# A decoder trunk on one core: gates and values of retention heads 1 to 7 as column pairs with seven-product blocks, and the retention's output product in two halves of such pairs

## The chip, the core and the metric

The kernel runs on one core of a Trainium2 chip. The metric is the device time of one execution, in microseconds (us), taken as the median of several runs. The core has a matrix engine (TensorE, PE in the profile; its weight loads are PEld), VectorE (DVE), ScalarE (ACT), GpSimd (POOL), SyncE (SP, which here only issues DMAs) and 16 DMA engines. Each engine takes its instructions in the order in which they stand in its own queue. A DMA is issued by an engine and moves data on its own; SP's DMAs are in queue q1 of the profile, POOL's in q0.

## What is computed

There are 256 tokens of 2048 features, all float32, and two layers: a retention layer with a squared-ReLU MLP, then a latent attention layer (MLA) with another such MLP. The change is in the retention and in what joins it to the MLP. Cut to that:

```python
h = rms_norm(x, norm_mix[0])
proj = h @ w_in                                  # 2048 x 12288
q, k, v, gate = split(proj, [2048, 4096, 8192])  # 8 heads: 256 of q, 256 of k, 512 of v, 512 of gate
q = apply_rope(q, cos, sin); k = apply_rope(k, cos, sin) * 256**-0.5
scores = (q @ k.T) * decay[head]                 # per head, causal
o = rms(scores @ v)                              # per head, over its 512 columns
x = x + (silu(gate) * o) @ w_out                 # 4096 x 2048
x = x + square(relu(rms_norm(x, norm_mlp[0]) @ w1)) @ w2
```
`cos` and `sin` are taken of positions times inverse frequencies.

## The kernel before

Tokens stand in two tiles of 128. Every float32 product is made of three matmuls of a rounded format (fp32r): an operand is split into a high and a low part, and high x high, high x low and low x high are added up in PSUM. The activations are split once. The weights come from memory in chunks of 1 MB: `stream` (L177) or `quad` (L251) issue the load on SP into one of three `raw` buffers, ACT casts the high half (`wh`, L154), DVE subtracts it for the low half (`wl`, L155), 128 x 1024 at a time, into five buffers each, and PE multiplies.

There are three forms of product. `gemm` (L372) takes a block of 512 output columns, four rows of 128 of the contraction in a chunk, through `piece` (L204, matmuls at L215 to L217). `gemm_t` (L224) makes the transposed q and k of a head (L239, L243). `gemm_pair` (L300) takes two neighbouring column blocks together: one chunk is a 2 x 2 block of weights (two contraction rows by two column blocks), and `quad` multiplies it with the 2 x 2 block of the activations (two token tiles by two contraction rows). A plain block does this in 8 block products, 24 matmuls (L323 to L325). Where the block's index is in `SEVEN = (3, 5, 7)`, it is done by 7 products, 21 matmuls, after a Strassen-Winograd scheme: DVE makes sums of weight blocks (`u`, L283 to L288) and sums of activation blocks must be at hand (`with_sums`, L358). A pair has eight such blocks or more, all added up in PSUM: four banks `acc`, two banks `tp` for p1 and p5, and the double bank `at` for p6 and p7. At its end `pair_out` (L334) copies six banks out on ACT, makes the results on DVE with four operations of 128x512, and hands on every output block as a pair of parts to be added; `summed` (L351) adds them with four more.

The retention runs head by head (L633). Before, each head is `rg` (its gate, `gemm`), `rq` and `rk` (`gemm_t`), `rv` (its values, `gemm`). The weights of a head are eight chunks of 1 MB for `rg` and `rv` and four for `rq` and `rk`. `ret_rope` (L564) turns q and k by a table, `ret_scores` (L584) multiplies them, `ret_out` (L605) multiplies scores and values, normalises, multiplies with the gate and transposes into `y`. After the eight heads `gemm_blocks` (L384) multiplies `y` with the output weights, four column blocks one by one, and `into_next` (L433) adds the result to x, stores x to the DRAM tiles `x_home`, and makes the split and transposed activations of the MLP. The MLP (L680) is made of pairs, four groups of two `u` pairs and two `d` pairs. All `d` pairs but the last group's add their results to `x_home` by accumulating DMAs on POOL's queue (L736); before the last group `x_tiles` (L117) loads x back.

At the start (`start`, L551) the first head's gate product is joined with the loads of the transposed x (`x0t`, L535) and their split. POOL loads the positions and the constants `cst` (L110, L111), then computes the angles of the rotary table (`sincos`, L451), 512 elements wide and some twenty operations long; ACT takes the sine (`tr_sc`, L487), DVE scales it, PE transposes it, and `rope_tab` (L493) is ready for the first head's rotation.

What runs when is set in two steps. The program writes the products one after another, and puts the work that hangs on their results in a queue with due times: `later(n, f)` (L81) runs `f` n chunks of weights later, `tick` counts chunks, `need` runs queued work until an item exists. A scheduler then moves the instructions of each engine by what they wait for. Tiles of one tag share buffers in turn: `f2k` has 14, `act` 24, `us` 2.

Of the kernel before, what the change touches and what calls it, by code (L numbers as in the profile page):

```python
# [20 lines left out]
P = 128  # L21
# [29 lines left out]
def yoco(ctx: ExitStack, tc: tile.TileContext, a):  # L51
# [58 lines left out]
    nc.gpsimd.dma_start(pos_i, a["pos"])  # L110
    nc.gpsimd.dma_start(cst[:, :C_MASK], a["cst"][:, :C_MASK])  # L111
# [35 lines left out]
    def square_sum(src, acc, name):  # L147
        junk = pool.tile([P, 512], BF16, tag="junk", bufs=2, name=f"{name}_sq")
# [151 lines left out]
    def gemm_pair(w, chunk0, act, kinds, name, done):  # L300
# [150 lines left out]
    def sincos(inv, w, name):  # L451

        n = NT * w
        ang = f2k([NT, w], f"{name}_ang")
# [30 lines left out]
        def finish():  # L485
            sc = f2k([2, NT, w], f"{name}_sc")
            nc.scalar.activation(sc.rearrange("p i t w -> p i (t w)"), r, AF.Sin)  # L487
            return sc
# [4 lines left out]
    rope_tab = pool.tile([P, 2, S], F32, tag="us", bufs=2, name="rope_tab")  # L493
# [23 lines left out]
    def scale_tables():  # L517
# [9 lines left out]
        later(1, turn)  # L527


    act0, r0, y_act, ret_sc, mla_sc = [], [], [], [], []  # L530

    def first_inputs(c):
# [5 lines left out]
        act0.append(v)  # L538

# [11 lines left out]
    def start(half):  # L551
        first_inputs(half)
        if half == 0:
            ret_tables()
        if half == 7:
            nc.sync.dma_start(cst[:, C_MASK:], a["cst"][:, C_MASK:])
            nc.sync.dma_start(gpe, a["gpe"])
# [4 lines left out]
            later(20, mla_tables)  # L562

# [41 lines left out]
    def ret_out(h, s, v, gate):  # L605
# [18 lines left out]
        def turn():  # L624
            for k2 in range(2):
                tp = transposed(lambda t, j: ys[t][:, (2 * k2 + j) * P : (2 * k2 + j + 1) * P], f"ytp{h}{k2}")
                yt = act_tile(f"y{h}{k2}")
                split_act(yt, tp)
                y_act.append(yt)

        later(2, turn)

    for h in range(RH):  # L633
        qk, gate, v, s = [], [], [], []
        wait = 7 if h == 0 else 0

        def gated(acc, h=h, gate=gate, wait=wait):
            src = acc
            if wait:
# [4 lines left out]
            def silu():  # L644
                for t in range(NT):
                    g = f2k([512], f"gate{h}{t}")
                    nc.scalar.activation(g, src[t], AF.Silu, scale=r0[t])
                    gate.append(g)

            later(wait, silu)  # L650

        def valued(acc, h=h, v=v, s=s, gate=gate):
            for t in range(NT):
                vh = f2k([512], f"vh{h}{t}", F32R)
                vl = f2k([512], f"vl{h}{t}", F32R)
                split(vh, vl, acc[t], r0[t])
# [421 lines left out]
```

## Time and profile before

| | |
|---|---|
| median of 3 runs | 2529.87 us (2526.89 to 2533.35) |
| profiled execution: its own time | 2532.54 us |
| profiled execution: span | 2530.4 us |
| PE | 2498.0 us busy (99%), 11794 matmuls |
| DVE | 1889.2 us (75%) |
| ACT | 1445.9 us (57%) |
| POOL | 220.6 us (9%) |

Where the stages begin, from the starts of PE's matmuls:

| stage | starts at us | lasts us |
|---|---|---|
| head 0: rg, rq, rk, rv | 5.3, 40.6, 51.8, 63.1 | 35.3, 11.3, 11.3, 27.4 |
| heads 1 to 7: rg, rq, rk, rv each | 90.5 to 583.4 | 24.7, 11.3, 11.3, 23.1 |
| output product (ro) | 583.4 | 179.7 |
| first MLP | 763.1 | 693 |
| MLA | 1456 | 380 |
| second MLP | 1835.8 | 694 |

The time outside the span is 2532.54 - 2530.4 = 2.1 us. In a line of groups or of a timeline, L is the line of the kernel, then come the engine, the operation, `out<-in` by the names of the tiles, their shapes, and after the bar or in brackets the idle time before it and what ended that. A matmul's time in a row is from its start to its modelled end, and matmuls overlap; the cost of one is the distance of two starts.

### The profile page before, as it was taken

The page shows a single profiled execution, that of the slowest core. Times are in us where ns is not written, and L with a number is a line of the kernel's source. Part 1 is how long each engine was busy: PE and PEld are TensorE (multiplying, and loading weights), DVE is VectorE, ACT ScalarE, POOL GpSimd, SP SyncE. Part 2 cuts the span into 40 slices and gives each one's busy share as a digit, 9 for nine tenths or more (in the row PEclk, how much of TensorE's full clock was granted, in tenths as well). Part 3 has the DMA queues.
Part 4 walks back from the last instruction along what each step waited for, and adds up shares of the span by engine and source line. Part 5 has one row for each costly group of instructions (what it writes and reads, how often), then busy time and mean ns, then how long its engine had stood idle before and what let it go on. Part 6 is the DMA issues. An engine that isn't in the chain of part 4 may idle for free.

```text
span 2530.4 us, 31172 instructions
## 1 busy us (share of the span) xinstructions
PE 2498.0 (99%) x11794; PEld 2096.4 (83%) x11794; DVE 1889.2 (75%) x2430; ACT 1445.9 (57%) x1993; POOL 220.6 (9%) x285
## 2 busy tenths in 40 slices
PE   7999999999999999999999999999999999999999
PEld 6888888888888888888878888998888888888787
DVE  6555555554558988889879866887689888898896
ACT  5544444444446656657556666565566566575663
POOL 6300000000000020110110011101000201101100
PEclk9999999999999999999999999999999999999999
DMA  7555455555655586685775555435555856857754
GB/s 264 178 185 181 173 189 182 184 205 190 207 194 189 192 260 203 210 249 192 241 249 188 212 208 179 163 125 200 191 186 191 260 206 219 248 190 223 255 196 165
DMA packets 89814, 513.67 MB, mean 203 GB/s; under 512 B 10528, under 2 KB 11696, under 8 KB 36416
## 3 DMA queue, kind: packets, MB, share of 16 engines
q1 hardware_dynamic: 71136, 471.69, 52.5%
q0 software_dynamic: 18384, 39.94, 7.6%
q8 instruction: 92, 1.51, 0.2%
q14 instruction: 58, 0.48, 0.1%
q10 hardware_dynamic: 144, 0.05, 0.0%
HBM read 478.09 MB, written 33.55 MB: 202 GB/s over the span
## 4 chain that ended last, share of the span: by engine, by line
PE 84%; DVE 8%; DMA 4%; ACT 3%; issue 1%; POOL 1%; SPq 0%; ACTq 0%; DVEq 0%; POOLq 0%
PE u_c L324 6%; PE u_c L325 6%; PE u_c L323 6%; PE d_c L324 5%; PE d_c L325 5%; PE d_c L323 5%; PE rq_acc L243 2%; PE rg_acc L217 2%; PE ro_acc L217 2%; PE ro_acc L215 2%; PE ro_acc L216 2%; PE rg_acc L215 2%; PE rg_acc L216 2%; PE rv_acc L216 2%; PE rv_acc L217 2%; PE rv_acc L215 2%
## 5 line engine op out<-in xcount | busy, mean ns | idle before, releaser
L155 DVE TENSOR_TENSOR u_wl<-u_raw,u_wh 128x1024 fp32r<-128x1024 f32 (+1 forms) x256 | 279.1, 1120 | 46.3 <-ACT u_wh L154 45.8
L155 DVE TENSOR_TENSOR d_wl<-d_raw,d_wh 128x1024 fp32r<-128x1024 f32 (+1 forms) x256 | 283.5, 1133 | 28.1 <-ACT d_wh L154 27.1
L324 PE MATMUL u_c<-u_wl,n 128*128 128x512 f32 x736 | 287.8, 391 | 5.2 <-DVE u_wl L155 5.2
L323 PE MATMUL u_c<-u_wh,n 128*128 128x512 f32 x736 | 288.7, 392 | 0.0
L154 ACT CAST u_wh<-u_raw 128x1024 fp32r<-128x1024 f32 (+1 forms) x256 | 238.6, 977 | 85.2 <-PE u_c L325 34.4
L325 PE MATMUL u_c<-u_wh,n 128*128 128x512 f32 x736 | 287.1, 390 | 0.0
L154 ACT CAST d_wh<-d_raw 128x1024 fp32r<-128x1024 f32 (+1 forms) x256 | 239.6, 991 | 58.0 <-DMA d_raw<-in_mlp_w 28.5
L324 PE MATMUL d_c<-d_wl,hid 128*128 128x512 f32 x644 | 251.5, 391 | 3.8 <-DVE d_wl L155 3.7
L323 PE MATMUL d_c<-d_wh,hid 128*128 128x512 f32 x644 | 252.0, 391 | 0.0
L325 PE MATMUL d_c<-d_wh,hid 128*128 128x512 f32 x644 | 250.8, 389 | 0.0
L154 ACT CAST u_wh<-u_u 128x1024 fp32r<-128x1024 f32 x96 | 98.3, 1048 | 165.2 <-DVE u_u L288 136.3
L154 ACT CAST d_wh<-d_u 128x1024 fp32r<-128x1024 f32 x84 | 84.7, 1047 | 162.9 <-DVE d_u L288 159.0
L324 PEld LDWEIGHTS u_c<-u_wl,n 128*128 128x128 f32 x736 | 138.6, 188 | 35.9 <-DVE u_wl L155 7.8
L325 PEld LDWEIGHTS u_c<-u_wh,n 128*128 128x128 f32 x736 | 138.6, 188 | 28.7
L323 PEld LDWEIGHTS u_c<-u_wh,n 128*128 128x128 f32 x736 | 138.5, 188 | 28.3
L155 DVE TENSOR_TENSOR u_wl<-u_u,u_wh 128x1024 fp32r<-128x1024 f32 x96 | 115.5, 1223 | 46.4 <-ACT u_wh L154 46.4
L324 PEld LDWEIGHTS d_c<-d_wl,hid 128*128 128x128 f32 x644 | 121.0, 188 | 31.2 <-DVE d_wl L155 6.8
L325 PEld LDWEIGHTS d_c<-d_wh,hid 128*128 128x128 f32 x644 | 120.9, 188 | 24.9
L323 PEld LDWEIGHTS d_c<-d_wh,hid 128*128 128x128 f32 x644 | 120.9, 188 | 24.7
L155 DVE TENSOR_TENSOR ro_wl<-ro_raw,ro_wh 128x1024 fp32r<-128x1024 f32 x64 | 78.4, 1225 | 82.1 <-ACT ro_wh L154 81.9
L155 DVE TENSOR_TENSOR rg_wl<-rg_raw,rg_wh 128x1024 fp32r<-128x1024 f32 (+1 forms) x68 | 81.6, 1208 | 62.6 <-ACT rg_wh L154 62.6
L155 DVE TENSOR_TENSOR d_wl<-d_u,d_wh 128x1024 fp32r<-128x1024 f32 x84 | 99.8, 1222 | 36.0 <-ACT d_wh L154 36.0
(378 smaller groups left out, 6217.6 us busy)
## 6 DMA issues: line engine op xcount, KB each, us to landing
u_raw<-in_mlp_w SPq DMA_DIRECT2D x128, 1024.0 KB, 5.5
d_raw<-in_mlp_w SPq DMA_DIRECT2D x112, 1024.0 KB, 4.9
rv_raw<-in_ret_w_gv SPq DMA_DIRECT2D x32, 1024.0 KB, 4.8
ro_raw<-in_ret_w_out SPq DMA_DIRECT2D x32, 1024.0 KB, 4.8
rg_raw<-in_ret_w_gv SPq DMA_DIRECT2D x28, 1024.0 KB, 4.8
uq_raw<-in_mla_w_uq SPq DMA_DIRECT2D x24, 768.0 KB, 4.2
rq_raw<-in_ret_w_qk SPq DMA_DIRECT2D x16, 1024.0 KB, 4.8
rk_raw<-in_ret_w_qk SPq DMA_DIRECT2D x16, 1024.0 KB, 4.8
```

The lines of the kernel that those rows point to most:

```text
L154: nc.scalar.copy(h, src)
L155: nc.vector.tensor_tensor(l, src, h.bitcast(F32), op=ALU.subtract)
L215: nc.tensor.matmul(acc[t], ah, rh, start=k == 0, stop=False)
L216: nc.tensor.matmul(acc[t], ah, rl, start=False, stop=False)
L217: nc.tensor.matmul(acc[t], al, rh, start=False, stop=k == nk - 1)
L243: nc.tensor.matmul(acc[f], wh[:, cols], a.rearrange("p i s -> p (i s)"), start=k == 0, stop=k == nk - 1)
L323: nc.tensor.matmul(dst, ah, bh, start=n == 0, stop=False)
L324: nc.tensor.matmul(dst, ah, bl, start=False, stop=False)
L325: nc.tensor.matmul(dst, al, bh, start=False, stop=n == total[key] - 1)
```

## The change

Six things change. (1) The gate and value columns of heads 1 to 7 are laid side by side, so that one `gemm_pair`, named rp1 to rp7, makes both; blocks 3, 5 and 7 of its eight take seven products. The order in a head is now rq, rk, rp. Head 0 keeps `rg0` and `rv0`. (2) For these blocks the first activations need sums, made by `sum_up` some chunks after the load. (3) The output product is made of pairs, in two halves. The first half takes heads 0 to 3 (ro00, ro01, three seven-product blocks each), is written after rk of head 4, and its results go to `x_home` by accumulating DMAs (`to_home`); the second half (ro10, ro11, two such blocks each) is written after the last head and goes into x (`into_x`). (4) Therefore `x_home` gets x at the start, by eight DMAs from DRAM to DRAM on POOL's queue, and x for the second half comes from `x_home`. (5) `x_tiles` loads x block by block, two chunks apart, in place of all at once. The first `u` pair of the first MLP takes seven products in two blocks in place of three. (6) At the start, `pos_i`, `cst` and `gpe` are loaded on SP after the fourth half chunk of `rg0`; `sincos` is written with the sixth half in place of the first; its buffers are `act` tiles; `rope_tab` has its own buffer; the square sums' scrap buffer is one in place of two; and the table's transposition is due one chunk later.

```diff
--- before.py
+++ after.py
@@ -107,20 +107,33 @@
     nc.gpsimd.memset(neg_half, -0.5)
     warm = small(1, "warm")
     nc.scalar.copy(warm, neg_half[:, 0:1])
-    nc.gpsimd.dma_start(pos_i, a["pos"])
-    nc.gpsimd.dma_start(cst[:, :C_MASK], a["cst"][:, :C_MASK])
 
     dram = ctx.enter_context(tc.tile_pool(name="dr", bufs=1, space=bass.MemoryType.DRAM))
     x_home = [[dram.tile([P, 512], F32, name=f"xh_{t}_{b}") for b in range(NB)] for t in range(NT)]
     x = [[None] * NB for t in range(NT)]
 
-    def x_tiles(home, name):
-
-        for b in range(NB):
+    def x_tiles(name):
+
+
+        def bring(b):
             both = act_tile(f"x_{name}{b}", F32)
             for t in range(NT):
                 x[t][b] = both[:, t].rearrange("p i s -> p (i s)")
-                nc.gpsimd.dma_start(x[t][b], home(t, b))
+                nc.gpsimd.dma_start(x[t][b], x_home[t][b])
+
+        for b in range(NB):
+            later(2 * b, lambda b=b: bring(b))
+
+    def to_home(c, p):
+
+        for j in range(2):
+            for t in range(NT):
+                for part in c[t][j]:
+                    nc.gpsimd.dma_start(x_home[t][2 * p + j], part, accum_op=ALU.add)
+
+    def into_x(done, c, p):
+        for j in range(2):
+            later(2 * j, lambda j=j: done(2 * p + j, [c[t][j] for t in range(NT)]))
 
     def gain(col):
         return gains[:, col : col + 1]
@@ -145,7 +158,7 @@
         return r.rearrange("p (t i h) -> p t i h", t=NT, i=len(sizes))
 
     def square_sum(src, acc, name):
...
             need(act, i + 1)
-            quad(w, chunk0 + i, act[i], mm, f"{name}{i}")
+            v, more = act[i]
+            quad(w, chunk0 + i, (v, more if kinds[i] else None), mm, f"{name}{i}")
...
+        def f2k(shape, name):
+            return shaped(act_tile(name, F32).rearrange("p j i s -> p (j i s)"), shape)
...
-    rope_tab = pool.tile([P, 2, S], F32, tag="us", bufs=2, name="rope_tab")
+    rope_tab = pool.tile([P, 2, S], F32, name="rope_tab")
...
-        later(1, turn)
+        later(2, turn)
...
+        sums0.append(None)
+        if c in SEVEN:
+
+            def sum_up():
+                for j in range(2):
+                    nc.scalar.activation(t[:, j], t[:, j], AF.Copy, scale=gain(G_MIX0 + 2 * c + j))
+                sums0[c] = with_sums(t, f"a0s_{c}")
+
+            later(9 + c, sum_up)
 
...
     def start(half):
         first_inputs(half)
-        if half == 0:
+        if half == 3:
+            nc.sync.dma_start(pos_i, a["pos"])
+            nc.sync.dma_start(cst, a["cst"])
+            nc.sync.dma_start(gpe, a["gpe"])
+        if half == 5:
             ret_tables()
         if half == 7:
-            nc.sync.dma_start(cst[:, C_MASK:], a["cst"][:, C_MASK:])
-            nc.sync.dma_start(gpe, a["gpe"])
             for b in range(NB):
                 later(2 + b, lambda b=b: load_x(b))
             later(5, scale_tables)
             later(12, lambda: mla_sc.append(sincos(cst[:, C_INVM : C_INVM + 32], 32, "tm")))
             later(20, mla_tables)
+            for b in range(NB):
+                for t in range(NT):
+                    later(20 + b, lambda t=t, b=b: nc.gpsimd.dma_start(x_home[t][b], x_in(t, b)))
...
                 tp = transposed(lambda t, j: ys[t][:, (2 * k2 + j) * P : (2 * k2 + j + 1) * P], f"ytp{h}{k2}")
                 yt = act_tile(f"y{h}{k2}")
-                split_act(yt, tp)
-                y_act.append(yt)
+                more = None
+                if len(y_act) in (SEVEN if h < RH // 2 else SEVEN[1:]):
+                    u = f2k([2, S], f"yu{h}{k2}")
+                    nc.scalar.copy(u, tp)
+                    split_act(yt, u)
+                    more = with_sums(u, f"y{h}{k2}")
+                else:
+                    split_act(yt, tp)
+                y_act.append((yt, more))
 
         later(2, turn)
+
+    ss = [small(NB, f"ss1_{t}") for t in range(NT)]
+    act, r = [], []
+    into_n1 = into_next(ss, [G_MLP0], [act], r, "n1", True)
+    halves = [[], []]
+
+    def ret_projected(h, qk, gate, v, s):
+
+        wait = 0 if h else 7
+
+        def keyed(acc):
+            ret_rope(acc, qk, f"rk{h}", max(wait - 4, 0))
+            later(max(wait - 4, 0) + 1, ret_scores(h, qk, s))
+
+        gemm_t(a["ret_w_qk"], h * 2, act0, KD, f"rq{h}", lambda acc: ret_rope(acc, qk, f"rq{h}", max(wait - 2, 0)))
+        gemm_t(a["ret_w_qk"], (RH + h) * 2, act0, KD, f"rk{h}", keyed)
+
+    def ret_valued(src, h, s, v, gate):
+        for t in range(NT):
+            vh = f2k([512], f"vh{h}{t}", F32R)
+            vl = f2k([512], f"vl{h}{t}", F32R)
+            split(vh, vl, src[t], r0[t])
+            v.append((vh, vl))
+        later(1, lambda: ret_out(h, s, v, gate, halves[h // 4]))
+
+    def ret_out_half(i):
+
+        w = a["ret_w_out"]
+        if i:
+            x_tiles("ro")
+        for p in range(2):
+            first = SEVEN[1:] if i else SEVEN
+
+            def done(c, p=p):
+                into_x(into_n1, c, p) if i else to_home(c, p)
+
+            gemm_pair(w, p * 16 + 8 * i, halves[i], [k in first for k in range(8)], f"ro{i}{p}", done)
 
     for h in range(RH):
         qk, gate, v, s = [], [], [], []
-        wait = 7 if h == 0 else 0
-
-        def gated(acc, h=h, gate=gate, wait=wait):
-            src = acc
-            if wait:
+        if h == 0:
+
+            def gated(acc, gate=gate):
                 src = [f2k([512], f"gate_raw{t}") for t in range(NT)]
                 for t in range(NT):
                     nc.scalar.copy(src[t], acc[t])
 
-            def silu():
-                for t in range(NT):
-                    g = f2k([512], f"gate{h}{t}")
-                    nc.scalar.activation(g, src[t], AF.Silu, scale=r0[t])
-                    gate.append(g)
-
-            later(wait, silu)
-
-        def valued(acc, h=h, v=v, s=s, gate=gate):
+                def silu():
+                    for t in range(NT):
+                        g = f2k([512], f"gate0{t}")
+                        nc.scalar.activation(g, src[t], AF.Silu, scale=r0[t])
+                        gate.append(g)
+
+                later(7, silu)
+
+            gemm(a["ret_w_gv0"], 0, act0, KD, 512, "rg0", gated, start)
+            ret_projected(h, qk, gate, v, s)
+            gemm(
+                a["ret_w_gv0"], 4, act0, KD, 512, "rv0",
+                lambda acc, v=v, s=s, gate=gate: ret_valued(acc, 0, s, v, gate),
+            )
+            continue
+
+        def paired(c, h=h, gate=gate, v=v, s=s):
+            c = summed(c)
             for t in range(NT):
-                vh = f2k([512], f"vh{h}{t}", F32R)
-                vl = f2k([512], f"vl{h}{t}", F32R)
-                split(vh, vl, acc[t], r0[t])
-                v.append((vh, vl))
-            later(1, lambda: ret_out(h, s, v, gate))
-
-        def keyed(acc, h=h, qk=qk, s=s, wait=wait):
-            ret_rope(acc, qk, f"rk{h}", max(wait - 4, 0))
-            later(max(wait - 4, 0) + 1, ret_scores(h, qk, s))
-
-        gemm(a["ret_w_gv"], h * 4, act0, KD, 512, f"rg{h}", gated, None if h else start)
-        gemm_t(
-            a["ret_w_qk"], h * 2, act0, KD, f"rq{h}",
-            lambda acc, h=h, qk=qk, wait=wait: ret_rope(acc, qk, f"rq{h}", max(wait - 2, 0)),
-        )
-        gemm_t(a["ret_w_qk"], (RH + h) * 2, act0, KD, f"rk{h}", keyed)
-        gemm(a["ret_w_gv"], (RH + h) * 4, act0, KD, 512, f"rv{h}", valued)
-
-    ss = [small(NB, f"ss1_{t}") for t in range(NT)]
-    act, r = [], []
-    x_tiles(x_in, "ro")
-    gemm_blocks(
-        a["ret_w_out"], lambda b: b * 8, y_act, 32, "ro", into_next(ss, [G_MLP0], [act], r, "n1", True)
-    )
+                nc.scalar.activation(c[t][0], c[t][0], AF.Silu, scale=r0[t])
+                gate.append(c[t][0])
+            ret_valued([c[t][1] for t in range(NT)], h, s, v, gate)
+
+        ret_projected(h, qk, gate, v, s)
+        if h == RH // 2:
+            ret_out_half(0)
+        need(r0, NT)
+        while None in [sums0[k] for k in SEVEN]:
+            run_first()
+        gemm_pair(a["ret_w_gv"], (h - 1) * 8, list(zip(act0, sums0)), [k in SEVEN for k in range(8)], f"rp{h}", paired)
+    ret_out_half(1)
 
 
     def mlp(layer, act, r, done):
@@ -710,11 +781,12 @@
                 later(1, lambda: turn(1))
 
             for p in range(f0 // 2, (f0 + nf) // 2):
+                seven = SEVEN if p or layer else SEVEN[1:]
                 gemm_pair(
-                    w1, p * 8, act, [i in SEVEN for i in range(8)], f"u{layer}_{p}", lambda c, p=p, up=up: up(c, p)
+                    w1, p * 8, act, [i in seven for i in range(8)], f"u{layer}_{p}", lambda c, p=p, up=up: up(c, p)
                 )
             if last:
-                x_tiles(lambda t, b: x_home[t][b], f"mlp{layer}")
+                x_tiles(f"mlp{layer}")
             for p in range(2):
                 if last and p:
                     for b in (2, 3):
@@ -726,14 +798,7 @@
                     continue
 
                 def add(c, p=p, last=last):
-                    for j in range(2):
-                        b = 2 * p + j
-                        if last:
-                            later(2 * j, lambda b=b, j=j: done(b, [c[t][j] for t in range(NT)]))
-                            continue
-                        for t in range(NT):
-                            for part in c[t][j]:
-                                nc.gpsimd.dma_start(x_home[t][b], part, accum_op=ALU.add)
+                    into_x(done, c, p) if last else to_home(c, p)
 
                 gemm_pair(w2, p * 32 + 2 * f0, blocks, kinds, f"d{layer}_{gi}{p}", add)
             f0 += nf
@@ -976,7 +1041,7 @@
 
     ss = [small(NB, f"ss3_{t}") for t in range(NT)]
     act, r = [], []
-    x_tiles(lambda t, b: x_home[t][b], "wo")
+    x_tiles("wo")
     gemm_blocks(a["mla_w_o"], lambda b: b * 4, o_act, KD, "wo", into_next(ss, [G_MLP1], [act], r, "n3", True))
 
     def finish(b, acc):
@@ -1040,6 +1105,9 @@
     gpe = np.concatenate([g["mla_k_pe_norm"], g["mla_q_pe_norm"][0]])
     cst, dec = _constants()
     w_in = g["ret_w_in"][0]
+    gv = np.stack(
+        [w_in[:, -RH * RDV :].reshape(D, RH, RDV), w_in[:, 2 * RH * RDK : -RH * RDV].reshape(D, RH, RDV)], axis=2
+    )
     arrays = {
         "x": x,
         "xt": x.T.reshape(KD, P, S).transpose(1, 0, 2),
@@ -1049,8 +1117,9 @@
         "cst": cst,
         "decay": dec,
         "ret_w_qk": _chunks(w_in[:, : 2 * RH * RDK], RDK, 8),
-        "ret_w_gv": _chunks(np.concatenate([w_in[:, -RH * RDV :], w_in[:, 2 * RH * RDK : -RH * RDV]], axis=1), RDV),
-        "ret_w_out": _chunks(g["ret_w_out"][0], 512),
+        "ret_w_gv0": _chunks(gv[:, 0].reshape(D, 2 * RDV), RDV),
+        "ret_w_gv": _quads(gv[:, 1:].reshape(D, (RH - 1) * 2 * RDV)),
+        "ret_w_out": _quads(g["ret_w_out"][0]),
         "mla_w_kv_up": _chunks(g["mla_w_kv_up"], 512),
         "mla_w_dq": _chunks(g["mla_w_dq"][0], 512),
         "mla_w_uq": _chunks(g["mla_w_uq"][0], Q_NB),
```

More of the change, by code (lines that the diff above doesn't have):

```diff
@@ L147, in square_sum @@
     def square_sum(src, acc, name):
-        junk = pool.tile([P, 512], BF16, tag="junk", bufs=2, name=f"{name}_sq")
+        junk = pool.tile([P, 512], BF16, tag="junk", bufs=1, name=f"{name}_sq")
         nc.scalar.activation(junk[:, : src.free_size()], src, AF.Square, accum_out=acc)
@@ L603, in ret_scores, with ret_out @@
         return go
-    def ret_out(h, s, v, gate):
+    def ret_out(h, s, v, gate, y_act):
         o = two_banks(f"o{h}")
```

8 lines of the change are left out of this document (4 added, 4 removed).

## The prediction

> **What bounds the kernel now.** I read the busy shares first, then PE's waits after the first 26 us, then the windows of three stages, then the timelines of the start.
>
> ```profile
> PE 2498.0 (99%) x11794; PEld 2096.4 (83%) x11794; DVE 1889.2 (75%) x2430; ACT 1445.9 (57%) x1993; POOL 220.6 (9%) x285
> ...
> PE u_c L324 <- DVE u_wl L155: 5.2, 4, 2.2
> PE d_c L324 <- DVE d_wl L155: 3.7, 5, 1.0
> ```
> The first line is the profile page, the others are PE's waits (us in total, times, longest). PE works 99% of the span, and what it waits for in the MLP pairs is always the low half of a weight, which VectorE (DVE) makes. So the number of matmuls sets the time, and DVE is the next limit. How near it is, the windows say (busy us and count of PE, PEld, DVE, ACT, POOL; then the granted clock, DMA share, GB/s):
>
> ```profile
> 0.00:26.00 26.00, 13.18 (x32) 9.32 (x33) 18.21 (x23) 15.40 (x29) 18.80 (x21) 0.80 0.90 311
> 90.00:583.00 493.00, 493.00 (x2420) 415.92 (x2419) 280.44 (x348) 221.66 (x275) 31.84 (x61) 1.00 0.54 186
> 763.00:1456.00 693.00, 688.41 (x3098) 567.79 (x3097) 598.81 (x699) 442.62 (x590) 54.53 (x68) 1.00 0.66 216
> ```
> In heads 1 to 7 of the retention PE never stops and DVE is busy 280.44/493 = 57%. In the first MLP, built from pairs, it is 598.81/693 = 86% with few PE stalls. A head that goes over to pairs moves towards the second row. In the first 26 us the DMA engines are 90% busy and PE works half of the time. The timelines show why, and what the change touches there:
>
> ```profile
> 1.64 10.38 SPq L192 DMA_DIRECT2D rg_raw<-in_ret_w_gv  x9
> 12.06 2.98 SPq L535 DMA_DIRECT2D x0t<-in_xt  x6
> ...
> 17.69 0.79 PE L215 MATMUL rg_acc<-rg_wh,a 128*128 128x512 f32 x1 [6.76 <-ACT a L157]
> 23.72 0.63 PE L217 MATMUL rg_acc<-rg_wh,a 128*128 128x512 f32 x1
> 24.14 0.46 PE L215 MATMUL rg_acc<-rg_wh,a 128*128 128x512 f32 x1
> 25.14 0.40 PE L216 MATMUL rg_acc<-rg_wl,a 128*128 128x512 f32 x1
> 25.37 0.39 PE L217 MATMUL rg_acc<-rg_wh,a 128*128 128x512 f32 x1
> ...
> 7.73 1.20 POOL L456 TENSOR_SCALAR tr_ang<-cst,pos_f 128x128 f32<-128x128 f32 x2 [5.23 <-DMA cst<-in_cst]
> 44.84 1.50 POOL L483 TENSOR_SCALAR tr_rr<-tr_rr 128x512 f32<-128x512 f32 x1
> ...
> 65.96 0.63 ACT L487 ACTIVATE tr_sc<-tr_rr 128x512 f32<-128x512 f32 x1
> ```
> SP sends the x0t loads behind nine weight issues, so PE stalls 6.76 us, then runs cold: matmuls start 0.427 us apart up to 24.14 and 0.23 us apart after. POOL needs cst, then computes the rotary angles until 44.84 + 1.50 = 46.34; the Sin that reads them starts only at 65.96, so the angles have about 18 us in hand.
>
> **The change, term by term.** The sum is made against the profiled execution, 2532.54 us; the median is 2529.87, 2.67 lower. 0.3%, about what can be told from no change, is 7.6 us.
>
> 1. Matmuls. A seven-product block takes 21 matmuls instead of 24. Heads 1 to 7 have 3 such blocks each: 7 x 3 x 3 = 63 fewer. The output product has 3 + 3 + 2 + 2 = 10: 30 fewer. u0_0 loses one such block: 3 more. Net 90 fewer. In steady state 220.35 to 220.58 is one matmul; over a whole head the spacing is 0.2267. 90 x 0.2267 = **-20.4**.
>
> 2. The start. The changed program puts three things differently. The x0t loads stand between the weight loads of rg0, so the 6.76 us stall should go, and rg0 should end near 34 instead of 40.6. cst goes from POOL's queue, where it landed at 7.5, to the 13th load of SP's, behind 3.34 MB. POOL's queue begins with eight copies of x into x_home (2.1 MB), which share the DMA engines with it. And on ACT the Sin stands directly before the cast of rk0's first weight: ACT takes its instructions in order, so PE gets no rk0 weight until the angles are done; their 18 us in hand are gone. The price: in the start 256 KB land every 0.65 us (x0t at 17.11, 17.80, 18.46, 19.13), the first load at 3.96, so 3.34 MB end at about 12.2. The copies move 4.2 MB counting both ends, 5.8 us at the 360 GB/s that SP's queue reaches in the MLP window (132.65 MB in 53.1% of 693 us) or 10.8 at the 194 GB/s of POOL's (16.78 MB, 12.5%). They may lie wholly ahead of cst or behind it. So the angles start between 12.2 and 23.0; I take 19, a 7 us copy ahead. They take 38.6 as before, or 33.3 if each operation takes the shortest time that its form shows; I take 37. End: 19 + 37 = 56, then Sin, a cast, and the first rk0 matmul near 58 where it stood at 51.84: +6.2. PE then has idled some 12 us and starts cold: 14 matmuls x (0.427 - 0.2267) = +2.8. rv0 lasts 27.4 us against a steady 23.1, and 3.4 of that is PE waiting for the same table work, which is now done earlier: -3.4. Together **+5.6**; bounds -8 (12.2 + 33.3, no cold start) and +14 (23.0 + 38.6, cold).
>
> The row on the cold clock bears on a rule. In the Trainium skill, *TensorE: Matmul & The Clock Gate*, "Part 1: The HAM clock gate", full clock returns after about 3.4 us of sustained work and is lost after as long an idle window. Here it took 6.4 us (17.69 to 24.14), so the row is used; by the page's figure the cold start would be an estimated 1.6 and the sum 1.2 lower.
>
> 3. Pair hand-overs in the retention. DVE work per head: a seven-product block adds the sums of weights (1.22 + 2 x 0.69) and one and a half more subtractions (1.22 + 0.69), 4.5 in all, three times; the pair's end adds eight operations of 0.69. Today a head is 280.44/7 = 40 us of DVE in 493/7 = 70.4; after, 40 + 13.5 + 5.5 + 1 (odd copies) = 60 in 70.4 - 9 x 0.2267 = 68.4, 88%, beside the MLP's 86%. Stalls there sum to 8.9 us over some 60 pairs, 0.15 each; the worse ones, where a d pair follows a d pair, cost about 0.8. rp1 to rp7 and the four output pairs are 11 hand-overs: 0 (no stall in heads 1 to 7 today) to 9. I take **+4**, above the mean, because the output of head h stands only 64 matmuls (11.3 us) behind its pair: eight times 0.69, two 0.75 for the split values and four weights' 1.22 make 11.9 of DVE work to get by in that time.
>
> 4. The first half of the output product now sends 16 accumulate DMAs, and the second half's x loads come from x_home. In the MLP such DMAs land after 5.3 to 9.9 us and hold their buffers meanwhile; there PE hardly waits. Where a burst of loads collides with weights (the window of x_mlp, 89.0 us against 85.3 for a normal two pairs) it costs 3.7. So 0 to 6: **+3**, nearest to that row.
>
> 5. The x_mlp loads go out by twos over some time instead of as a burst. The bursts cost 4.0 and 3.1 us in stalls (1276 and 2349). In the changed order the last two tiles still come together: **-3**, half; -6 to 0.
>
> 6. The last output pair hands over to u0_0, whose first blocks need x: ro's end is 0 today, d's last stage costs 1.0 to 1.4, so **+1** (0 to 4).
>
> Everything else (buffers of sincos, one junk buffer, rope_tab of its own) costs nothing: ACT is 45% busy in the retention and the junk buffers are written by ACT alone, one after another. If that cover were gone a square sum (0.63) would wait for the next, under 1 us a head.
>
> Sum: -20.4 + 5.6 + 4 + 3 - 3 + 1 = -9.8. 2532.54 - 9.8 = 2522.7; on the median **2520.1**.
>
> **Rivals.**
>
> A. The start is worse: the copies come wholly first, the angles end at 62 or later, term 2 is +14, sum -1.4, time **2528.5**. For it: the DMA engines are 90% busy there, and a queue beside another takes its share. The Trainium skill, *DMA: Bandwidth & Descriptors*, "Queues, rings and completion order", has each DMA engine take turns between queues by packet; by that the copies delay cst by about their own time, which agrees with 7 us and speaks against an undisturbed cst. No row of before has a DRAM-to-DRAM copy. Chance 0.17.
>
> C. The start is gentle: copies late or cheap, angles from 15 in 35 us, end 50, rk0 at 52: term 2 is 0.2 + 2.8 - 3.4 = -0.4, sum -15.8, time **2514**. For it: half of POOL's operations show a shorter time of the same form (1.28 and 1.85 for the same subtraction), the short ones where DVE was idle. The Trainium skill, *SBUF — State Buffer*, "SBUF: two separate sides", says a DVE operation with two SBUF inputs and a GpSimd operation that reads SBUF shut each other out, which those rows agree with; in the new start DVE is busier then, which speaks against it. Chance 0.20.
>
> B. Slower: DVE becomes the bound at the pair hand-over. The 11.9 us of DVE work against 11.3 us of matmuls does not fit, the transposes of o and the next weights' subtractions queue behind each other, and every one of the 11 hand-overs costs 3 us (0.6 of overrun and two subtractions of 1.22 that stand in front). Then term 3 is 33 instead of 4: **2549**. It decides from (2537.5 - 2520.1 + 4) / 11 = 2.0 us a hand-over. For it: 88% average, and the chain is serial with ACT's copies. Against: the u pairs do as much per block and lose 0.15. Chance 0.18.
>
> That the change does not cut the matmuls is excluded by its instruction counts.
>
> **How the numbers follow.** The main case has 0.45; its own range is 2510 to 2531, of it 0.28 below 2522.3 and 0.17 within 0.3%. C adds 0.20 faster; A 0.11 same and 0.06 slower; B 0.18 slower. Faster 0.48, same 0.28, slower 0.24. The range reaches from 2504 (C with the low ends of terms 3 to 5) to 2546 (B at 2.7 us a hand-over); some 0.05 lie below and 0.12 above.
>
> **What will show it.** Term 1: 11,704 matmuls. Term 2: POOL's wait for cst, the end of tr_rr, and PE's wait before rk0's first matmul, 12 us by the main case, under 5 by C, over 16 by A. Term 3: DVE's share from 68 to 583 (about 88%) and PE's waits on low halves, or on o and the transposes; over 20 us in sum is B. Terms 4 and 5: PE waits near the middle output pairs and near the x_mlp loads. The prediction is wrong if PE's waits in heads 1 to 7 exceed 15 us, or if the wait at rk0 is absent.

## The result and the profile after

The changed kernel takes 2518.38 us (median of 6 runs, 2515.45 to 2520.94), the kernel before 2526.65 us in the runs beside it (6 runs, 2522.09 to 2533.35). The ratio is 0.9965, with a 95% interval of 0.9949 to 0.998: 5 to 13 us faster. The forecast was 2520.1, from a median before of 2529.87: a gain of 9.8 us was forecast, 8.3 us were measured.

The page's line of busy times for the changed kernel:

```profile
PE 2475.7 (98%) x11704; PEld 2077.5 (83%) x11704; DVE 2062.4 (82%) x2692; ACT 1532.9 (61%) x2138; POOL 236.8 (9%) x307
```

PE's waits in it after the first 26 us (us in total, times, longest):

```profile
PE rk_acc L256 <- ACT rk_wh L167: 9.7, 1, 9.7
PE sc L626 <- DVE rk_q L610: 6.7, 4, 3.7
PE d_c L337 <- DVE d_wl L168: 1.6, 4, 0.7
PE u_c L337 <- DVE u_wl L168: 0.3, 1, 0.3
```

The 90 matmuls are gone (11704 for 11794). Two waits are new: 9.7 us at the first matmul of rk0, and four waits at the scores (`sc`), which wait for the rotated k. The waits on low halves in the MLP pairs, 8.9 us before, are 1.9. The windows of the same three stages, and of the retention with the first output half inside (columns as before):

```profile
0.00:26.00 26.00, 17.31 (x57) 12.69 (x58) 11.96 (x21) 14.05 (x25) 8.51 (x18) 0.93 0.92 309
96.60:755.10 658.50, 651.76 (x3126) 546.01 (x3126) 544.90 (x693) 382.10 (x502) 38.85 (x66) 1.00 0.57 197
755.10:1445.90 690.80, 688.57 (x3109) 568.32 (x3108) 603.64 (x711) 446.67 (x601) 54.94 (x70) 1.00 0.67 219
```

In the retention DVE went to 544.90/658.5 = 83%, and PE stands still for 6.7 us there.

The profiled execution of before (2532.54) is near the slow end of its runs, that of the changed kernel (2515.45) is the fastest of its runs, so the two traces differ by 17.1 us where the medians differ by 8.3. A second profile of the changed kernel, taken with a later comparison (2524.72), is at the slow end of its own runs; beside those the kernel before took 2531.12 us, so the whole level was 4 to 5 us higher there. By stage:

| | before | changed | changed, second profile |
|---|---|---|---|
| end of rv0 | 90.5 | 96.6 | 97.0 |
| from there to the end of the output product | 672.6 | 658.5 | 662.1 |
| from there to the end of the span | 1767.3 | 1758.6 | 1763.9 |

So the start lost 6.1 to 6.5 us, and everything after it won.

The start of the changed kernel, in the timelines of POOL, ACT and PE:

```profile
1.29 4.31 POOL L594 DMA_DIRECT2D xh<-in_x  x8 [0.45 <-issue]
21.86 1.20 POOL L474 TENSOR_SCALAR tr_ang<-cst,pos_f 128x128 f32<-128x128 f32 x2 [16.27 <-DVE pos_f L532]
56.54 0.61 POOL L501 TENSOR_SCALAR tr_rr<-tr_rr 128x512 f32<-128x512 f32 x1
...
57.19 0.63 ACT L505 ACTIVATE tr_sc<-tr_rr 128x512 f32<-128x512 f32 x1 [15.74 <-POOL tr_rr L501]
57.73 1.03 ACT L167 CAST rk_wh<-rk_raw 128x1024 fp32r<-128x1024 f32 x1
...
58.80 0.80 PE L256 MATMUL rk_acc<-a,rk_wh 128*128 128x512 f32 x1 [9.73 <-ACT rk_wh L167]
```

POOL issues the eight copies, waits 16.27 us, and computes the angles until 57.15. ACT waits 15.74 us for them with the sine and casts rk0's first weight right after. PE waits for that cast. In the trace's DMA landings cst is there at 20.17; the positions as floats, which the first operation also needs, come from one DVE instruction at 21.59.

### The profile page after: what moved, and what is told of

Its sections match the earlier page's. It is cut to its first block, busy times and chain, and to the rows that moved or that the text cites. A ratio compares the mean times of both kernels' runs of the same rounds, so it can differ in the third digit from the quotient of the medians.

```text
span 2513.7 us, 31410 instructions
## 1 busy us (share of the span) xinstructions
PE 2475.7 (98%) x11704; PEld 2077.5 (83%) x11704; DVE 2062.4 (82%) x2692; ACT 1532.9 (61%) x2138; POOL 236.8 (9%) x307
## 4 chain that ended last, share of the span: by engine, by line
PE 83%; DVE 7%; DMA 4%; ACT 3%; POOL 2%; issue 1%; SPq 0%; ACTq 0%; DVEq 0%; POOLq 0%
PE u_c L337 7%; PE u_c L338 7%; PE u_c L336 7%; PE d_c L337 5%; PE d_c L338 5%; PE d_c L336 5%; PE rp_c L338 3%; PE rp_c L337 3%; PE rp_c L336 3%; PE ro_c L337 2%; PE ro_c L338 2%; PE ro_c L336 2%; PE u_p L338 2%; PE u_p L337 2%; PE u_p L336 2%; DMA d_raw<-in_mlp_w 2%
## 5 line engine op out<-in xcount | busy, mean ns | idle before, releaser
L167 ACT CAST rp_wh<-rp_raw 128x1024 fp32r<-128x1024 f32 x112 | 106.9, 972 | 75.0 <-PE rp_c L338 45.5
L168 DVE TENSOR_TENSOR rp_wl<-rp_raw,rp_wh 128x1024 fp32r<-128x1024 f32 x112 | 121.7, 1120 | 8.0 <-ACT rp_wh L167 6.4
```

The lines of the kernel that those rows point to most:

```text
L167: nc.scalar.copy(h, src)
L168: nc.vector.tensor_tensor(l, src, h.bitcast(F32), op=ALU.subtract)
```

## Experiments: the start

My theory was that the late angles hold ACT, and ACT holds PE. Four kernels were run together on one chip: three take one thing away each, the fourth all three. Beside them the kernel before took 2528.21 us (11 runs).

**The sine late.** A zero bias made from r0 moves the sine behind the square sums on ACT:

```diff
-            nc.scalar.activation(sc, r, AF.Sin)
+            nc.scalar.activation(sc, r, AF.Sin, bias=bias)
...
-        sc = ret_sc[0]()
+        none = small(1, "none")
+        nc.vector.tensor_scalar(none, r0[NT - 1], 0.0, None, op0=ALU.mult)
+        sc = ret_sc[0](none)
```

> The changed kernel with one thing different: the sine takes a zero bias computed from r0, so that on ACT it stands behind the square sums, far behind the casts of rk0, instead of directly before them; cst and the copies stay where they are. Theory (ACT, taking its instructions in order, holds rk0's weights back until the angles are done): PE's 9.7 us wait before rk0 goes, rk0's first matmul moves from 58.8 to about 48, rk0 lasts 11.5 instead of 14.3 us because PE is not cold; rv0 may take back up to 3.4 us for the table. Gain over the changed kernel 10 to 13 us, to about 2506. Rival (the weights of rk0 are late from memory, and ACT's wait only covers that): rk0 starts after 54 and the gain is under 4 us.

Measured 2510.68 us, ratio 0.9924 (0.9908 to 0.994). The first rk0 matmul, in PE's timeline, and the first operation of the angles on POOL:

```profile
49.70 0.40 PE L256 MATMUL rk_acc<-a,rk_wh 128*128 128x512 f32 x1
...
22.49 1.21 POOL L474 TENSOR_SCALAR tr_ang<-cst,pos_f 128x128 f32<-128x128 f32 x2 [16.90 <-DVE pos_f L532]
```

The angles are as late as ever, yet rk0 starts at 49.70 with no wait, rk0 lasts 11.1 us instead of 14.3, and rv0 ends at 84.3 instead of 96.6. In the changed kernel rk0's first chunk had landed at 38.04; the order on ACT held it back. The stages gain 12.3 us as expected. The time gains 7.7 by the medians (of two comparisons) and 10 by the ratios. The ratio's intervals are wide enough for 12.3; whether a part of the gain is lost further on, this run does not show.

**Stores in place of copies.**

```diff
             nc.sync.dma_start(x0, x_in(t, b))
+            nc.gpsimd.dma_start(x_home[t][b], x0)
...
-            for b in range(NB):
-                for t in range(NT):
-                    later(20 + b, lambda t=t, b=b: nc.gpsimd.dma_start(x_home[t][b], x_in(t, b)))
```

> The changed kernel with the eight copies of x from DRAM to DRAM replaced by stores of the x tiles that the square sums load anyway, which come behind the angles on POOL's queue. Theory (the copies take the DMA engines from cst and from the first weights): cst lands near 14 instead of 20.2, the angles end near 51, rg0 ends near 33 instead of 36.6, rk0 starts near 52 instead of 58.8: a gain of about 6.5 us, to about 2512. Rival (cst is late because it is the 13th load on SP's queue and its conversion stands behind other work on DVE): cst lands after 18, gain under 2 us.

cst lands at 14.32 instead of 20.17, so the eight copies cost cst 5.85 us (the prediction took 7). The angles start at 16.04, rk0 at 53.2, rv0 ends at 91.0: 5.6 us earlier. PE still waits 9.8 us before rk0, as rg0 ends earlier too. The time is 2517.61, ratio 0.9952 (0.9937 to 0.9967): beside the changed kernel's 0.9965 only some 3 us, with overlapping intervals. The place of cst behind eleven other loads of SP's queue costs the rest: 14.32 against 8.25 in the next run.

**cst first.**

```diff
+    nc.gpsimd.dma_start(pos_i, a["pos"])
+    nc.gpsimd.dma_start(cst, a["cst"])
...
-            nc.sync.dma_start(pos_i, a["pos"])
-            nc.sync.dma_start(cst, a["cst"])
```

> The changed kernel with the positions and cst loaded by POOL's queue ahead of the copies, as in the kernel before. Theory: the angles start near 9 and end near 45 (POOL's first operation starts at 7.7 in the kernel before, and takes 35 to 38.6 us from there), the sine is then no longer late for ACT, rk0 starts where rq0 ends, near 48, and rk0 is not cold: gain 10 to 13 us, as with the sine late. Rival (the start is bound by the copies and the weights alone): rg0 and rk0 stay where they are, gain under 3 us.

Measured 2512.37 us, ratio 0.9928 (0.9911 to 0.9944). The angles run from 9.19 to 47.38, later than the expected 45, and the sine still stands before rk0's cast, but now waits only 2.69 us:

```profile
47.41 0.63 ACT L507 ACTIVATE tr_sc<-tr_rr 128x512 f32<-128x512 f32 x1 [2.69 <-POOL tr_rr L503]
47.95 1.03 ACT L169 CAST rk_wh<-rk_raw 128x1024 fp32r<-128x1024 f32 x1
```

rk0 starts at 52.1, not at 48, because rg0 ends later (40.2 instead of 36.6). The loss thus needs both: cst behind the weights and the copies, and the sine ahead of a cast. Undoing either one wins most of it back.

**All three.**

> The changed kernel with all three: cst first, stores in place of copies, the sine late. Theory: rg0 ends near 33 and rk0 starts near 44, no wait for the angles: gain 14 to 18 us over the changed kernel, to about 2502. Rival (what is saved in one place is waited for in the next, at the rotation table in rv0): the stages up to the end of rv0, 96.6 in the changed kernel, end after 86, gain under 10 us.

Measured 2506.7 us, ratio 0.991 (0.9895 to 0.9925). rg0 ends at 32.9, rk0 starts at 45.5, rv0 ends at 81.6: the stages gain 15.0 us, and by the ratios the time gains some 14, as expected.

## Experiments: the scores

The prediction put 4 us on the hand-over of pairs, on the ground that DVE would be 88% busy. Where the changed kernel really waits, DVE's timeline in rp7 shows (second profile of the changed kernel, then PE):

```profile
620.30 0.78 DVE L601 TENSOR_TENSOR rk_u<-rk_acc,rk_u 128x256 f32<-128x256 f32 x2
625.66 1.22 DVE L296 TENSOR_TENSOR rp_u<-rp_raw 128x1024 f32<-128x1024 f32 x1 [4.58 <-DMA rp_raw<-in_ret_w_gv]
...
629.67 0.68 DVE L607 TENSOR_TENSOR rk_q<-rk_u,rope_tab 128x512 f32<-128x512 f32 x1
...
631.15 0.42 DVE L610 TENSOR_TENSOR rk_q<-rk_q,rk_v 128x256 f32<-128x256 f32 x1
...
631.71 1.19 PE L626 MATMUL sc<-rq_q,rk_q 128*128 128x256 f32 x2 [4.47 <-DVE rk_q L610]
```

DVE is idle for 4.58 us. Its next instruction is the first sum of weights of block 3 (L296), whose chunk has not landed, and the rotation of k, which has all that it needs, stands behind it. PE reaches the scores 27 matmuls of rp (6.1 us) behind rk and waits. It is a wait in DVE's order for a transfer, not a load on DVE. The chunk was issued at 617.97 and landed at 625.63, 7.7 us, beside six loads of x for the second output half (1.5 MB, issued from 614.04 to 616.84; four of them were still on their way when the chunk was issued and landed by 621.53). In rp2 a chunk took 4.7 us, and DVE idled 1.41.

Three kernels test this. The first two ran on one chip with a repetition of the changed kernel, which took 2523.10 us, ratio 0.9962 (0.9948 to 0.9975); the kernel before took 2531.12 us there.

> The changed kernel once more, on the chip of the next three, to compare them with. Expected 2518 us, with rg0 31, rk0 starting near 59 and the scores waiting 6 to 8 us in sum. If the small waits on low halves differ from the first profile of it (3.2 us in sum) by more than 3 us, they are what moves the time from one execution to the next.

The repetition had the same waits in the start (rk0 at 59.2) and 7.7 us at the scores. Its waits on low halves in the MLP pairs are 5.7 us against 1.9, 3.8 us more, so the bound of 3 us is passed: these small waits are a part of what moves the time from one execution to the next.

**The scores one chunk later.**

```diff
-            later(max(wait - 4, 0) + 1, ret_scores(h, qk, s))
+            later(max(wait - 4, 0) + 2, ret_scores(h, qk, s))
```

> The changed kernel with the scores due one chunk later, so that in PE's order they stand 48 instead of 27 matmuls behind rk. Theory (PE waits at the scores because the rotated k comes from DVE more than 27 matmuls, 6.1 us, after rk): the waits at the scores, 6.7 us in sum, go, and nothing takes their place: gain 6 to 8 us. Rival (DVE is the bound there, and what PE does not wait for at the scores it waits for at the next weights' low halves): gain under 2 us.

Measured 2514.99 us, ratio 0.9935 (0.9922 to 0.9947): 8.1 us faster than the repetition beside it. The windows from the end of rv0 to the end of the output product, of the repetition, then of this run:

```profile
97.00:759.10 662.10, 653.55 (x3126) 547.27 (x3125) 546.47 (x695) 381.64 (x502) 40.64 (x68) 1.00 0.58 197
```

```profile
96.50:749.80 653.30, 653.10 (x3132) 547.32 (x3131) 543.86 (x694) 382.43 (x504) 41.21 (x68) 1.00 0.58 199
```

8.8 us less, PE without a gap, and DVE does the same 544 us. DVE still idles 3.47 us before L296 in rp7, but nobody waits for it. The rival, that the wait would only move to the low halves, falls.

**More work for DVE at every hand-over.**

```diff
             c = summed(c)
+            for t in range(NT):
+                for block in c[t]:
+                    nc.vector.tensor_tensor(block, block, block, op=ALU.max)
```

> The changed kernel with four more DVE operations of 128x512 (the maximum of a block with itself, which changes nothing) behind the sums of each of the seven rp pairs: 2.75 us more in the chain of every hand-over. My theory (the hand-over has a margin, DVE is not the bound): 0 to 6 us more in all. Rival B of the prediction (DVE bound at the hand-over, whose 11.9 us do not fit 11.3): every one of the seven costs its 2.75, some 15 to 20 us more.

Measured 2514.61 us, ratio 0.9931 (0.9919 to 0.9944): 28 operations more, and 8.5 us faster. The window from the end of rv0 to the end of the output product:

```profile
96.10:747.90 651.80, 651.49 (x3125) 545.88 (x3125) 559.47 (x720) 382.52 (x502) 41.81 (x66) 1.00 0.58 199
```

DVE's timeline in its rp7:

```profile
619.07 0.68 DVE L607 TENSOR_TENSOR rk_q<-rk_u,rope_tab 128x512 f32<-128x512 f32 x1
...
625.29 1.22 DVE L296 TENSOR_TENSOR rp_u<-rp_raw 128x1024 f32<-128x1024 f32 x1
```

The scheduler answered the added work with another order: the scores stand 24 matmuls behind rk, and on DVE the rotation stands ahead of L296. PE stands still for 0.3 us in that window although DVE is now 86% busy (559.47/651.8). So the added work has cost PE nothing there, and rival B falls: DVE is not the bound at the hand-over. That the kernel became faster was in neither expectation. The run does not give a clean price of DVE work, since the order changed with it.

**The loads of x later**, six chunks, with PE's order up to there unchanged:

```diff
-            later(2 * b, lambda b=b: bring(b))
+            later(2 * b + (6 if name == "ro" else 0), lambda b=b: bring(b))
```

> The changed kernel with the loads of x for the second half of the output product due six chunks later; the order on PE up to there is the same. Theory (in rp7 six loads of x, 1.5 MB, delay the chunk of block 3 from 4.7 to 7.7 us, DVE stops 4.6 us at the first sum of its weights, and the rotation of k, which stands behind it, makes the scores late): the stall in rp7 falls from 6.9 to about 2 us, as in rp2 and rp3, rp7 from 49.2 to 44.5; the other waits at the scores stay. 4 to 5 us faster than the changed kernel. Rival (the place in DVE's queue alone does it): rp7 stays above 47.

Measured 2519.07 us, ratio 0.9947 (0.9935 to 0.996), against 0.9962: some 4 us by the middle values, with overlapping intervals. In rp7 the chunk takes 4.9 us instead of 7.7, DVE and PE wait less, and rp7 lasts 44.8 us instead of 49.2:

```profile
621.83 1.22 DVE L296 TENSOR_TENSOR rp_u<-rp_raw 128x1024 f32<-128x1024 f32 x1 [1.69 <-DMA rp_raw<-in_ret_w_gv]
...
627.88 0.67 PE L626 MATMUL sc<-rq_q,rk_q 128*128 128x256 f32 x2 [1.59 <-DVE rk_q L610]
```

So in these executions 4.4 of the 8.8 us come from the loads of x meeting a chunk that DVE's order waits for, and the other 4.4 remain with that order; 5.2 us of waits at the scores are left. Both shares are of single executions: in the first profile of the changed kernel rp7 lasts 46.9 us.

## Experiments: x by blocks, and the price of a block

**x all at once again.** The changed kernel with `bring(b)` called directly, wherever `x_tiles` loads x:

> The changed kernel with x loaded all at once by x_tiles, as before, in place of block by block. Theory (the burst takes the DMA engines from the weights): the stages of u before the last d pairs go back from 84.8 to 88 to 89 us in both MLPs, 7 to 8 us more, and 0 to 2 more where x comes for the second half of the output product: 2526. Rival (the stalls of the burst were where they were by chance of the weights' order): under 2 us.

Measured 2528.76 us, ratio 0.9989 (0.9981 to 0.9998), 5.7 us slower than the repetition beside it. The window of the u stage before the last d pairs of the first MLP, of the repetition, then with the burst (columns as before):

```profile
1273.60:1358.70 85.10, 85.00 (x383) 70.26 (x382) 73.82 (x82) 53.67 (x69) 8.68 (x13) 1.00 0.73 243
```

```profile
1272.90:1361.60 88.70, 86.75 (x383) 71.41 (x382) 73.83 (x82) 53.96 (x69) 8.79 (x14) 0.98 0.69 233
```

The burst costs a stall and, in the clock column, 0.98 for 1.00: PE comes back cold. In the second MLP the stage took 86.1 us, no more than 86.9 in the repetition, so 88 came back in one MLP, not in both. The two traces differ by 1 us only (2525.68 and 2524.72); it is the timed runs that show the 5.7.

**The kernel before with x by blocks**, the only part of the change that it takes over (again at every place where `x_tiles` loads x):

> The kernel before with one part of the change alone: x_tiles loads x block by block, two chunks apart. Theory (the burst of x costs what its removal from the changed kernel costs, 5.7 us): the two u stages before the last d pairs fall from 89.0 and 88.2 to about 85, the time by 5 to 7 us, and so more than half of the gain of the whole change is this part. Rival (the burst only hurts where pairs fill the retention too): under 2 us.

Measured 2525.66 us, the kernel before beside it 2532.0; ratio 0.9973 (0.996 to 0.9985), 4 to 10 us. The same stage of the first MLP, in the kernel before, then with x by blocks:

```profile
1276.50:1365.50 89.00, 86.79 (x383) 71.38 (x383) 73.89 (x82) 53.98 (x69) 8.80 (x14) 0.98 0.69 233
```

```profile
1276.70:1362.30 85.60, 85.14 (x384) 70.29 (x383) 73.84 (x82) 53.68 (x70) 8.76 (x14) 1.00 0.73 242
```

It fell to 85.6 from 89.0, that of the second MLP to 84.8 from 88.2. This part needs no pairs in the retention, and alone it is worth, by the medians, three quarters of the change's net gain.

The traces also show how little of the burst was moved. In the changed kernel's first MLP the loads of the first two blocks are still issued at once, directly behind eight accumulating DMAs (1281.2 to 1282.9); only those of the last two blocks come later, at 1317.7 and 1324.0. Weights of 1 MB still take 6.5 to 8.4 us beside that, where the median of the u chunks is 5.4. What these DMAs still cost was not tried.

**Two seven-product blocks in place of three** in rp1 to rp7, with the scores one chunk later:

> The changed kernel with the scores due one chunk later, as in the run e7_sc_late, and with two instead of three seven-product blocks in each of rp1 to rp7. Theory (a matmul is worth its 0.2267 us where nothing else waits): 21 matmuls more, 4.8 us slower than e7_sc_late, each rp 0.68 us longer than its 43.0. Rival (DVE's load of the pairs costs time in small waits): the third block is worth less, under 2.5 us.

Ratio 0.9956 (0.9942 to 0.9969) at 2522.46 us, against 0.9935 with three (on another chip): 5 us by the ratios, with intervals that just overlap. In rp2, rp3, rp5 and rp6 the stage is 0.68 us longer, as expected; in the other three it is 0.19 to 0.44. The seven sum to 303.9 us instead of 300.2, 0.18 us for each of the 21 matmuls rather than 0.2267. So by the stages a third block is worth nearly its matmuls, and more than the rival's 2.5 us. A part of the 5 us is not theirs: the u stage of the first MLP took 89.4 us here, with x by blocks. Such a stall thus comes without the burst too, and one execution's stage is weak evidence for it; the timed runs of the two comparisons above carry the reading that the burst costs time.

**All that helps.** cst first, stores, the sine late, the scores one chunk later:

> The changed kernel with what the runs before point to: cst first, stores in place of copies, the sine late, the scores one chunk later. If the two savings add up (11 to 13 us in the start, 8 at the scores): about 20 us faster than the changed kernel, ratio to the kernel before 0.988. If the early start only lets PE wait elsewhere: above 0.990.

Measured 2502.3 us, the kernel before beside it 2532.0; ratio 0.9872 (0.9856 to 0.9888), 28 to 36 us faster than before; by the ratios some 23 us faster than the changed kernel, where 20 were expected. PE's longest wait in its profiled execution, 2494.31, the fastest of its four:

```profile
PE rg_acc L230 <- ACT a L172: 5.5, 1, 5.5
```

This is the wait for the first matmul of all. Neither the wait at rk0 nor that at the scores is left. This is the version to keep.

## Why the prediction was right, step by step

The time was right, and so was the sign; neither of its two signs of being wrong came (PE waits 6.7 us in heads 1 to 7, under 15, and the wait at rk0 is there). That the sum came so near is in part luck: errors of several terms cancel. Of the terms, the start was right in size and mechanism, x by blocks was right in mechanism and half its size, and the hand-overs came near their size for another reason than the one given.

1. Matmuls, -20.4. The 90 are gone. The run with two blocks in place of three gave 3.7 us for 21 of them in the rp stages, at which rate 90 are 16, and 5 us by the ratios, at which 90 are 21. In four of the seven pairs three matmuls cost 0.68 us, the price taken. So -20.4 is not contradicted, and not confirmed to better than that.

2. The start, +5.6. Measured +6.1 and +6.5, by the steps named: angles from 21.86 (19 taken, 12.2 to 23.0 bounded) for 35.3 us (37 taken), rk0 at 58.80 (58), rk0 3.0 us longer (2.8; the granted clock was 0.81 in it, and 0.5 of the 3.0 is a wait for a low half), -3.9 in rv0 (-3.4). The sine late shows the cause. The nearness of rk0 is luck in part: the angles began 2.9 us later than taken and went 1.7 faster. Four figures were wrong and did little: the 5.8 and 10.8 us of the copies are those of 2.1 MB at the two rates, not of the 4.2 MB that stand beside them (the copies cost cst 5.85); the time in hand before the sine was 19.6 us (46.34 to 65.96), not 18; of the 3.4 us in rv0 PE's waits for the table are only 1.9, with the granted clock at 0.50 behind them; and the bound +14 leaves out this -3.4, with which it is 11. What failed is the step that rg0 would lose its stall: the one of 6.76 us went, but five shorter ones came, 4.0 us in sum, because the copies delay the x0t loads that stand between the weights (the third landed at 16.63 instead of 10.74 with stores, where such stalls are 0.5 us in sum and rg0 lasts 25.8 us instead of 31.0). It ended at 36.6, not at 34; as PE then waited for the angles, this changed nothing in the sum, and made the wait 9.7 instead of 12.

3. Hand-overs, +4. The waits are there, but the step that DVE's 11.9 us of work would not fit 11.3 us failed. DVE was 83% busy, not 88%, it was idle while PE waited for it, and with more work for it, in another order, PE did not wait. In place of it: an instruction waiting for a chunk stood ahead of the rotation in DVE's order, 4.4 us. That this is near 4 is luck. (The 0.15 us a pair was also too low: the two MLPs have 32 pairs, not some 60, so 8.9 us are 0.28 each.)

4. Accumulate DMAs and x loads, +3. No PE wait lies at the accumulate DMAs of the first half, though they land after 6.0 to 11.1 us. The loads of x cost 4.4 us in the second profile, through the chain of point 3 in rp7: the mechanism, a collision with weights, was named, the size was 1.4 short, and the place was not foreseen.

5. x by blocks, -3. Worth 5.7 us when taken out of the changed kernel and 6.3 when put into the one before, by the medians: the term took half of the stalls (4.0 and 3.1), and by the medians nearly the whole of them went. It held that the last two tiles would still come together; it is the first two blocks that do, and the last two come 35 and 41 us behind them.

6. ro to u0_0, +1. No wait. Eight transposes of x moved into u0_0 (87.2 us for 85.7), from the output product.

Terms with their measured sizes: -20.4 + 6.3 + 4.4 + 4.4 - 6.0 + 0 = -11.3, beside -8.0 and -8.3 of the medians in the two comparisons. Points 3 to 6 were forecast at +5.0 together and came to +2.8, as the errors of 4 and 5 have opposite signs. Some 3 us of the sum are not found. They are less than the spread: the two profiled executions of the changed kernel differ by 9 us (2515.45 and 2524.72), 3.6 of it in the retention and 5.3 behind it. Of the 5.3, 3.8 are waits on low halves in the MLP pairs; what sets those was not tried.

Rivals: B falls by the run with more work for DVE. A and C were the two ends of term 2, and the case lay between. That the copies and SP's loads share the DMA engines (the Trainium skill, *DMA: Bandwidth & Descriptors*, "Queues, rings and completion order") agrees with cst landing 5.85 us earlier without the copies.

## What to carry to other kernels

Before moving a small transfer or a long side chain, look in whose in-order queue its consumer stands and what stands behind it: a sine whose input had been ready 19.6 us before it ran cost 12 us when it came to stand ahead of a cast. An engine that shows 83% busy can still be idle at the moment that counts; the idle column with its releaser, on the engine that PE waits for, tells load from order. Test the parts of a compound change alone: here loading x by blocks alone gave 6.3 us where the whole change gave 8, and four small changes of place gave some 20 more.

## What the runs showed of the hardware that I had not expected

In these runs the same chain of operations on POOL took between 35.4 and 41.8 us, and longer the more DVE worked beside it. From the windows over the angles: 35.4 us in the changed kernel with DVE 18.50 us busy (52%), 35.6 with stores (52%), 38.3 with cst first (80%), 38.7 before (81%), 39.7 with the sine late (83%), 41.8 with all three (88%). The timeline of the changed kernel shows single operations of one form, the first with DVE at work, the second while DVE waits:

```profile
36.92 2.35 POOL L489 TENSOR_SCALAR tr_part<-tr_kh 128x512 f32<-128x512 f32 x1
44.54 1.49 POOL L489 TENSOR_SCALAR tr_part<-tr_k 128x512 f32<-128x512 f32 x1
```

ACT is busy during the first and idle during the second too. But with cst first such an operation took 1.50 us at 38.42 with ACT busy throughout and DVE for 0.28 us, so ACT alone does not slow it. The Trainium skill, *SBUF — State Buffer*, "SBUF: two separate sides", has a DVE operation with two SBUF inputs and a GpSimd operation that reads SBUF shut each other out; these rows agree with it. An earlier start of the angles was thus partly given back: cst first began 12.7 us earlier and ended 9.8 earlier.
